# Four-layer network on one core: spilled and fresh expert pairs interleaved, fetched rows spread, gates in quarters, end of the layer and gmlp in a new order

## The chip, the cores and the metric

The kernel runs on one core of a Trainium2 chip. The metric is device time in microseconds (us) of one execution, as the median of several. A profiled execution of the same program gives the trace from which all rows below come. Engines are named as in the profile: PE is TensorE's matmul, PEld its weight load, DVE is VectorE, ACT is ScalarE, POOL is GpSimd, SP is SyncE, which here only starts transfers; a "q" behind a name is that engine's DMA queue.

## The reference

The network handles 512 tokens of width 1024 in fp32 through several layers. Two of its pieces matter. `peer` routes each token, by 8 heads and two sets of 128 sub-keys, to 16 experts a head; an expert's number is `i1 * 128 + i2`, and its first and second matrices are one row each of `expert_u` and `expert_v` (16384 rows).

```python
def peer(n, w_q, sub_keys_1, sub_keys_2, expert_u, expert_v):
    ...
        v1, i1 = lax.top_k(s1, PEER_TOPK)
        v2, i2 = lax.top_k(s2, PEER_TOPK)
        cand_s = (v1[..., :, None] + v2[..., None, :]).reshape(...)
        cand_i = (i1[..., :, None] * PEER_NKEYS + i2[..., None, :]).reshape(...)
        top_s, pos = lax.top_k(cand_s, PEER_TOPK)
        idx = jnp.take_along_axis(cand_i, pos, axis=-1)
        g = jax.nn.softmax(top_s, axis=-1)
        u_sel = jnp.take(expert_u, idx, axis=0)
        act = jax.nn.gelu(jnp.einsum('thkd,td->thk', u_sel, xc).astype(jnp.float32))
        v_sel = jnp.take(expert_v, idx, axis=0)
        return jnp.einsum('thk,thkd->td', (g * act).astype(xc.dtype), v_sel)
```

`gmlp_mixer` follows it in the next layer: `u = gelu(u_pre)`, `v = layer_norm(gelu(v_pre))`, `v` mixed over the tokens of a chunk by a lower-triangular matrix for each group, and `u * mixed` as the result.

## The kernel before

**Numbers and tiles.** Tokens stand in 4 blocks of 128. Each fp32 product is made of three matmuls on parts: `mm3` (L354 to L359) does hi x hi, lo x hi and hi x lo. Weights stream from HBM as 128 x 1024 tiles: SP starts the transfer into `raw` (3 buffers), ScalarE casts it to `whi` (L319), VectorE subtracts to `wlo` (L320); `whi` and `wlo` have 4 buffers each. `parts` (L486, L487) does the same for activations. The 16384 experts are handled as 128 tiles ("expert 0 to 127" below) of 128 rows each.

**Block 0's tokens are sparse.** For them each chosen row is fetched by an indirect DMA from POOL (L1429) into `row` (5 buffers, 4 fetches ahead), first from `u`, reduced against the token on VectorE (L1438), then from `v`, added into `acc` (L1446). There are 128 of each; `next(fetch)` advances this by one row.

**Blocks 1 to 3 (384 tokens) are dense.** Each of the 128 expert tiles is projected for all 384 tokens (24 matmuls of 384 columns into bank `pm` or `pt`), passed through gelu, multiplied by a dense table of gates `G` (mostly zeros), split into `zh` and `zl`, and multiplied by its tile of `w_v` into 6 banks (2 `pa`, 4 `pm`), 18 matmuls of 512 columns, which accumulate over all 128 experts.

**Leads.** While `peer_gates` works out scores, picks and gates, TensorE would have little to do, so `lead` projects the first LEAD = 104 experts there, and SP stores their gelu to a DRAM table `H` (a "spilled" expert). 102 of them are placed by a list of fill counts, the others by `while todo: lead()`. The picks (L1509 to L1512) find `ex`, the expert number of each of 16 picks among 50 candidates: `eq` compares, `oh` multiplies, `reduce_sum` adds over the candidates, which is here the axis with a step of 16 elements.

**The expert stage** (`peer_experts`) handles experts in pairs. `act(e)` loads gates for 8 experts at a time (1.5 MB, the first group in three parts), loads `zs` for four spilled experts at a time (768 KB, 2 buffers) or projects a fresh pair, and makes `zh`, `zl`. `out(e, b)` does the output matmuls. The loop does a pair's outputs, then `beside(3)` rows for a spilled pair and `beside(6)` for a fresh one, then `act(e + 4)`. Pairs 0 to 51 are spilled, 52 to 63 fresh.

**The end of the layer.** `end(b)` scales, norms (`two_norms`) and adds the residual for block b; `late[b]` transposes it (TensorE, L497), `behind` places these transpositions behind a block of `w3_gv` matmuls, and `begin(b)` starts those. In `gmlp` each of four rounds projects `u` (`fm`), takes its gelu, and mixes `v` by 128 x 128 matmuls (L1883) of `gmw`, for which POOL's `gmv` must be done.

**Order.** A scheduler sorts each engine's instructions ahead of time; an engine then runs them strictly in that order. A DMA started by ACT (`G`, `zs`) or SP (`raw`) waits in that engine's order for its buffer, and what stands behind it waits too.

Of the kernel before, what the change touches and what calls it, by code (L numbers as in the profile page):

```python
# [9 lines left out]
F32 = mybir.dt.float32  # L10
# [6 lines left out]
OP = mybir.AluOpType  # L17
# [268 lines left out]
class Builder:  # L286
# [169 lines left out]

    def tmb_block(self, st, x, ks, b, h, ps):
        n = len(ks)
        for i, k in enumerate(ks):
# [924 lines left out]
    def peer(self):  # L1384

        tc = self.tc
        GT, TS, NE, LEAD, N = 8, 16, 128, 104, S - P
        with tc.tile_pool(name="pe", bufs=1) as p0, tc.tile_pool(name="ped", bufs=1, space=DRAM) as pd, \
                ExitStack() as right:
            nT = self.nT  # L1390
            G = pd.tile([N // TS, P, NE, TS], F32, name="gates")
            H = pd.tile([LEAD // GT, P, GT, N], F32, name="lead")
            su = self.stream("w2_u")
            n0 = p0.tile([P, D], F32, name="n0")
            self.nc.sync.dma_start(n0, self.n0)
            with tc.tile_pool(name="pek", bufs=1) as p, tc.tile_pool(name="pet", bufs=2) as t2, \
                    tc.tile_pool(name="pey", bufs=2) as ty:

                todo = list(range(LEAD))

                def lead(i=0, n=1, fill=1):

                    r = None
                    for _ in range((i + 1) * fill // n - i * fill // n):
                        e = todo.pop(0)
                        z = p0.tile([P, N], F32, name="z", bufs=3)
                        ps = self.pm.tile([P, 512], F32, name="pm")
                        self.fm_half(su, e, nT, 8, ps, P, S)
                        r = self.nc.scalar.activation(z, ps[:, P:], AF.Gelu_apprx_tanh)
                        self.nc.sync.dma_start(H[e // GT, :, e % GT], z)  # L1410
                    return r
                fetch = self.peer_gates(p, t2, ty, p0, right, n0, nT, G, TS, NE, lead)
                while todo:
                    lead()
            with tc.tile_pool(name="pek", bufs=1) as p:
                self.peer_experts(p, nT, su, G, H, GT, TS, NE, LEAD, *fetch)

# [31 lines left out]
    def peer_gates(self, p, t2, ty, p0, right, n0, nT, G, TS, NE, lead):  # L1449
# [9 lines left out]
        v.tensor_copy(iob, iot[:, :, None].to_broadcast([P, NE, 2]))  # L1459
        ioc = p.tile([P, NC, 16], BF16, name="ioc")  # L1460
        v.tensor_copy(ioc, iot[:, 0:NC, None].to_broadcast([P, NC, 16]))

# [32 lines left out]
        def picks(b, fill, then=None):  # L1495
# [100 lines left out]

    def peer_experts(self, p, nT, su, G, H, GT, TS, NE, LEAD, pr, fetch):

# [4 lines left out]
        gf = self.rowload(p, "gf2", name="gf2")  # L1603
        acc, parts, left = {}, {}, [2 * P - 96]

        def beside(n):
            for _ in range(min(n, left[0])):
                next(fetch)
            left[0] = max(left[0] - n, 0)

        def act(e):

            if e % GT == 0:
                gt = act.gt = p.tile([P, N // TS, GT, TS], F32, name="G", bufs=2)
                for b in range(0, N // TS, 8 if e == 0 else N // TS):
                    c = b + 8 if e == 0 else N // TS
                    nc.scalar.dma_start(gt[:, b:c], G[b:c, :, e:e + GT, :].rearrange("b p e t -> p b e t"))
# [11 lines left out]
            v.tensor_tensor(z.rearrange("p k (b t) -> p k b t", t=TS), z.rearrange("p k (b t) -> p k b t", t=TS),  # L1629
                            act.gt[:, :, e % GT:e % GT + 2, :].rearrange("p b e t -> p e b t"), OP.mult)  # L1630
            hi, lo = (p.tile([P, 2, N], F32R, name=n, bufs=3) for n in ("zh", "zl"))
# [11 lines left out]

        act(0)
        act(2)
        for e in range(0, NE - 2, 2):
            for k in range(2):
                for b in range(1, NB):
                    out(e + k, b)
            beside(3 if e < LEAD else 6)  # L1650
            if e + 4 < NE:
                act(e + 4)
        beside(2 * P)

        ys = [t.rearrange("p b e t -> p (b e t)") for t in (p.tile([P, N // TS, GT, TS], F32, name="G", bufs=2)
                                                            for _ in range(2))]
        ys = [t[:, k * D:(k + 1) * D] for t in ys for k in range(2)]
        after = self.mod_norm(p, 0, 1, EPS3, ys, lambda: p.tile([P, 512], F32, name="q", bufs=2))
        load, begin = self.open_tmb("w3_gv", self.nT, range(8))
        late = []  # L1660

        def end(b):
            self.late = []
            late.append(self.late)
            for h in range(2):
# [3 lines left out]
                self.two_norms(b, h, ps, gf, EPS2, EPS3, ys[b], after.turn)  # L1669
        end(0)  # L1670
        self.behind(None, late[0])
        load(0), load(1)
        for b in range(1, NB):
            for e in (NE - 2, NE - 1):
                last = out(e, b)
                if b == NB - 1:
                    load(e - NE + 4)
            end(b)
        for b in range(1, NB):
            self.behind(begin(b - 1), late[b])  # L1680
        self.late = []
# [172 lines left out]
    def gmlp(self, q, hT, yT):  # L1854
# [504 lines left out]
```

## Time and profile before

| what | value |
|---|---|
| median of 3 runs | 3916.0 us (3914.04 to 3924.2) |
| profiled execution, its own time | 3914.44 us |
| its span in the trace | 3912.3 us, mean granted TensorE clock 0.973 |
| PE busy | 3672.4 us, 94% of the span, 18377 instructions |
| DVE busy | 2586.7 us, 66% |
| ACT busy | 1433.3 us, 37% |
| POOL busy | 598.4 us, 15% |
| chain that ended last | PE 66%, DVE 13%, DMA 9%, issue 7% |

The span is what the trace covers; the execution's own time is 2.1 us longer. Busy shares are means over stages with different limits. In the profile's 40 slices PE falls to 6 to 8 tenths between the 22nd and the 28th slice, about 2150 to 2740 us, which is the expert stage.

### The profile page before, as it was taken

To read this page: it belongs to the slowest core of one execution; us is meant where nothing else is said; L and a number is where in the kernel's file an instruction comes from. 1 tells how busy PE (TensorE), PEld (TensorE's weight loads), DVE (VectorE), ACT (ScalarE), POOL (GpSimd) and SP (SyncE) were. 2 spreads that over 40 slices of the span, in tenths; PEclk is the share of its full clock that TensorE was granted. 3 is DMA by queue.
4 is the path that set the end of the run, shared out by engine and by line. 5 is a ranking of instruction groups with operands and counts; after the bars stand their busy time and mean duration, and the time that the engine had idled before them with its cause. 6 is when DMAs were issued, how large, how long until landed. Compare 5 with 4: busy or idle time off the path is not lost.

```text
span 3912.3 us, 48482 instructions
## 1 busy us (share of the span) xinstructions
PE 3672.4 (94%) x18377; PEld 3101.9 (79%) x18377; DVE 2586.7 (66%) x4472; ACT 1433.3 (37%) x2122; POOL 598.4 (15%) x630
## 2 busy tenths in 40 slices
PE   8999999999999999999989687789998999999998
PEld 6777877777888888898989566678986787788887
DVE  5755748758645646999999677764457546755344
ACT  4422333323224633334546222233343334534231
POOL 1122100000000000254243444410001000010000
PEclk9999999999999999999999798899998999999999
DMA  4132433546233233289899998875432221133332
GB/s 154 65 100 82 124 96 111 177 127 191 81 97 97 92 98 113 89 282 320 306 351 377 363 338 313 321 271 171 145 108 84 84 73 55 49 94 95 97 97 76
DMA packets 221275, 622.20 MB, mean 159 GB/s; under 512 B 21052, under 2 KB 85165, under 8 KB 217841
## 3 DMA queue, kind: packets, MB, share of 16 engines
q1 hardware_dynamic: 120576, 398.18, 31.2%
q0 software_dynamic: 39776, 142.52, 10.1%
q10 hardware_dynamic: 60688, 78.40, 5.9%
q8 instruction: 144, 2.36, 0.2%
q14 instruction: 91, 0.74, 0.1%
HBM read 570.76 MB, written 48.26 MB: 158 GB/s over the span
## 4 chain that ended last, share of the span: by engine, by line
PE 66%; DVE 13%; DMA 9%; issue 7%; ACT 2%; POOL 2%; DVEq 0%; SPq 0%; POOLq 0%; ACTq 0%
PE pm L357 18%; PE pm L359 18%; PE pm L358 18%; DMA zs<-lead 4%; DVE wlo L320 3%; DMA raw<-in_w_up_dram 2%; DVE acc L1446 1%; POOL row L1429 1%; PE pa L358 1%; PE pa L359 1%; PE pt L359 1%; PE pt L357 1%; PE pt L358 1%; PE pa L357 1%; PE pt L497 1%
## 5 line engine op out<-in xcount | busy, mean ns | idle before, releaser
L319 ACT CAST whi<-raw 128x1024 fp32r<-128x1024 f32 x661 | 694.1, 1051 | 1617.0 <-PE pm L359 478.8
L320 DVE TENSOR_TENSOR wlo<-raw,whi 128x1024 fp32r<-128x1024 f32 x661 | 817.3, 1237 | 662.4 <-ACT whi L319 653.8
L357 PE MATMUL pm<-xTh,whi 128*128 128x512 f32 (+2 forms) x2784 | 1016.5, 366 | 35.1 <-ACT whi L319 21.0
L359 PE MATMUL pm<-xTh,wlo 128*128 128x512 f32 (+2 forms) x2784 | 1008.4, 363 | 13.4 <-DVE wlo L320 13.1
L358 PE MATMUL pm<-xTl,whi 128*128 128x512 f32 (+2 forms) x2784 | 1009.7, 363 | 2.2 <-DVE xTl L487 2.2
L357 PEld LDWEIGHTS pm<-xTh,whi 128*128 128x128 f32 x2784 | 531.1, 191 | 102.8 <-ACT whi L319 24.8
L359 PEld LDWEIGHTS pm<-xTh,wlo 128*128 128x128 f32 x2784 | 530.3, 191 | 82.2 <-DVE wlo L320 21.1
L358 PEld LDWEIGHTS pm<-xTl,whi 128*128 128x128 f32 x2784 | 531.7, 191 | 63.3 <-DVE xTl L487 2.8
L1429 POOL DMA_INDIRECT row<-in_u_rows_dram,rows x128 | 182.9, 1429 | 285.9 <-DVE row L1438 243.8
L1429 POOL DMA_INDIRECT row<-in_w_v_dram,rows x128 | 186.0, 1453 | 236.1 <-DVE acc L1446 208.4
L357 PE MATMUL pm<-whi,zh 128*128 128x512 f32 x512 | 204.3, 399 | 0.0
L358 PE MATMUL pm<-wlo,zh 128*128 128x512 f32 x512 | 203.1, 397 | 0.0
L359 PE MATMUL pm<-whi,zl 128*128 128x512 f32 x512 | 202.7, 396 | 0.0
L358 PE MATMUL pa<-wlo,zh 128*128 128x512 f32 x256 | 106.2, 415 | 71.4 <-DVE wlo L320 71.3
L1446 DVE SCALAR_TENSOR_TENSOR acc<-row,hw,acc 128x1024 f32<-128x1024 f32 x127 | 163.1, 1285 | 14.6 <-DMA row<-in_w_v_dram,rows 12.7
L357 PE MATMUL pm<-whi,xTh 128*128 128x512 f32 (+1 forms) x400 | 161.7, 405 | 7.3 <-ACT xTh L486 4.3
L1438 DVE SCALAR_TENSOR_TENSOR row<-row,n 128x1024 f32<-128x1024 f32 x128 | 154.4, 1219 | 18.5 <-DMA row<-in_u_rows_dram,rows 18.3
L359 PE MATMUL pm<-whi,xTl 128*128 128x512 f32 (+1 forms) x400 | 155.3, 389 | 0.0
L358 PE MATMUL pm<-wlo,xTh 128*128 128x512 f32 (+1 forms) x400 | 153.8, 385 | 0.0
L357 PE MATMUL pa<-whi,zh 128*128 128x512 f32 x256 | 101.9, 399 | 32.9 <-ACT zh L486 32.9
L358 PEld LDWEIGHTS pa<-wlo,zh 128*128 128x128 f32 x256 | 49.9, 195 | 89.9 <-DVE wlo L320 80.6
L1629 DVE TENSOR_TENSOR zs<-zs,G 128x768 f32<-128x768 f32 x52 | 47.5, 954 | 106.3 <-DMA zs<-lead 106.3
(652 smaller groups left out, 6330.7 us busy)
## 6 DMA issues: line engine op xcount, KB each, us to landing
raw<-in_w_v_dram SPq DMA_DIRECT2D x136, 512.0 KB, 6.7
raw<-in_w_u_dram SPq DMA_DIRECT2D x128, 512.0 KB, 4.9
raw<-in_w_m_dram SPq DMA_DIRECT2D x64, 512.0 KB, 3.5
raw<-in_w_up_dram SPq DMA_DIRECT2D x55, 512.0 KB, 3.5
raw<-in_w_ada_dram SPq DMA_DIRECT2D x48, 512.0 KB, 4.5
gates<-G ACTq DMA_DIRECT2D x24, 1024.0 KB, 7.5
G<-gates ACTq DMA_DIRECT2D x15, 1536.0 KB, 24.7
lead<-z SPq DMA_DIRECT2D x104, 192.0 KB, 6.1
```

The lines of the kernel that those rows point to most:

```text
L319: nc.scalar.copy(hi, src)
L320: (nc.gpsimd if u < self.aside else nc.vector).tensor_tensor(lo, src, hi.bitcast(F32), OP.subtract)
L357: mm(ps, lhsT=a[0], rhs=b[0], start=first, stop=False)
L358: mm(ps, lhsT=a[0], rhs=b[1], start=False, stop=False)
L359: return mm(ps, lhsT=a[1], rhs=b[0], start=False, stop=last)
L497: self.nc.tensor.transpose(ps[:, j, :], src[:, j * P:(j + 1) * P], self.ident)
L1429: nc.gpsimd.indirect_dma_start(r, None, tabs[e], bass.IndirectOffsetOnAxis(ap=idx[e][:, j:j + 1], axis=0))
L1438: v.scalar_tensor_tensor(r, r, 1.0, n0, op0=OP.mult, op1=OP.mult, accum_out=hs[:, j:j + 1])
L1446: v.scalar_tensor_tensor(acc, r, w[:, j:j + 1], acc, op0=OP.mult, op1=OP.add)
L1629: v.tensor_tensor(z.rearrange("p k (b t) -> p k b t", t=TS), z.rearrange("p k (b t) -> p k b t", t=TS), act.gt[:, :, e % GT:e % GT + 2, :] ...
```

## The change

- `lead` now covers 112 experts: all pairs n with n % 8 != 7 (`held`, 56 pairs). The 8 fresh pairs are 7, 15, ..., 63, one in each run of eight.
- `H` is stored and `zs` loaded by pairs (384 KB), `zs` in 6 buffers and three pairs ahead (`zload(e + 6)`). Gates of the next group of 8 experts come in four quarters over the group before (`gload`).
- The 160 rows of block 0 that are left for this stage are spread over pairs 0 to 59 by weights of 1 (spilled) and 2 (fresh). Block 0's `end(0)` stands at pair 60 in place of behind the loop.
- The three other `end(b)` stand behind all last outputs; each `begin(b)` is split in halves, and the transpositions of a block stand behind the first.
- `eq` and `oh` are laid out [16, candidates], so that the sum runs over neighbouring elements.
- `gmlp` does the four projections of `u` first, then the four mixes.

```diff
@@ begin, in open_tmb
-            return self.tmb_block(st, x, ks, b, 0, st.begun[b])
+            n = len(ks) // 2
+            yield self.tmb_block(st, x, ks, b, 0, st.begun[b], range(n))
+            self.tmb_block(st, x, ks, b, 0, st.begun[b], range(n, 2 * n))
...
@@ peer
-        GT, TS, NE, LEAD, N = 8, 16, 128, 104, S - P
+        GT, TS, NE, N = 8, 16, 128, S - P
+        held = [n for n in range(NE // 2) if n % 8 != 7]
...
-            H = pd.tile([LEAD // GT, P, GT, N], F32, name="lead")
+            H = pd.tile([len(held), P, 2, N], F32, name="lead")
...
-                todo = list(range(LEAD))
+                todo = [(k, n, c) for k, n in enumerate(held) for c in range(2)]
...
-                        self.nc.sync.dma_start(H[e // GT, :, e % GT], z)
+                        self.nc.sync.dma_start(H[k, :, c], z)
...
@@ peer_gates
-                eq = t2.tile([P, NC, 16], BF16, name="eq")
-                v.tensor_tensor(eq, ioc, tpf[:, h, None, :].to_broadcast([P, NC, 16]), OP.is_equal)
-                oh = t2.tile([P, NC, 16], F32, name="oh")
-                v.tensor_tensor(oh, eq, ci[:, h, :, None].to_broadcast([P, NC, 16]), OP.mult)
-                v.reduce_sum(ex[:, h, :], oh.rearrange("p c k -> p k c"), axis=AX.X)
+                eq = t2.tile([P, 16, NC], BF16, name="eq")
+                v.tensor_tensor(eq, ioc, tpf[:, h, :, None].to_broadcast([P, 16, NC]), OP.is_equal)
+                oh = t2.tile([P, 16, NC], F32, name="oh")
+                v.tensor_tensor(oh, eq, ci[:, h, None, :].to_broadcast([P, 16, NC]), OP.mult)
+                v.reduce_sum(ex[:, h, :], oh, axis=AX.X)
...
@@ peer_experts
+        def gload(e, n, c):
...
+            if e not in gts:
+                gts[e] = p.tile([P, N // TS, GT, TS], F32, name="G", bufs=2)
+            b = slice(N // TS // n * c, N // TS // n * (c + 1))
+            nc.scalar.dma_start(gts[e][:, b], G[b, :, e:e + GT, :].rearrange("b p e t -> p b e t"))
+
+        def zload(e):
+            if e // 2 in held:
+                zs[e] = p.tile([P, 2, N], F32, name="zs", bufs=6)
+                nc.scalar.dma_start(zs[e], H[held.index(e // 2)])
...
-            if e % GT == 0:
-                gt = act.gt = p.tile([P, N // TS, GT, TS], F32, name="G", bufs=2)
-                for b in range(0, N // TS, 8 if e == 0 else N // TS):
...
-            if e < LEAD:
-                if e % 4 == 0:
-                    act.zs = p.tile([P, 4, N], F32, name="zs", bufs=2)
-                    nc.scalar.dma_start(act.zs, H[e // GT, :, e % GT:e % GT + 4])
-                z = act.zs[:, e % 4:e % 4 + 2]
-            else:
+            g0 = e - e % GT
+            gload(g0 + GT, GT // 2, e % GT // 2)
+            zload(e + 6)
+            z = zs.pop(e, None)
+            if z is None:
...
-            beside(3 if e < LEAD else 6)
...
+        due = [0]
+        for e in range(0, NE - GT, 2):
+            due.append(due[-1] + (1 if e // 2 in held else 2))
+        rows = 2 * P - 96
...
+            n = e // 2
+            if n + 1 < len(due):
+                for _ in range(rows * due[n + 1] // due[-1] - rows * due[n] // due[-1]):
+                    next(fetch)
+            elif n + 1 == len(due):
...
+                ys = [pr.tile([P, D], F32, name="row", bufs=5) for _ in range(NB)]
+                after = self.mod_norm(p, 0, 1, EPS3, ys, lambda: p.tile([P, 512], F32, name="q", bufs=2))
+                end(0)
+                self.behind(None, late[0])
...
         for b in range(1, NB):
             for e in (NE - 2, NE - 1):
-                last = out(e, b)
+                out(e, b)
                 if b == NB - 1:
                     load(e - NE + 4)
+        for b in range(1, NB):
             end(b)
         for b in range(1, NB):
-            self.behind(begin(b - 1), late[b])
+            half = begin(b - 1)
+            self.behind(next(half), late[b])
+            for _ in half:
+                pass
...
@@ gmlp
+        us = []
         for n in range(4):
             pu = self.fm(st, n, hT, 8)
-            u = tmp()
-            self.gelu2(u, pu, tmp)
+            us.append(tmp())
+            self.gelu2(us[n], pu, tmp)
+        for n, u in enumerate(us):
             ps = self.pa.tile([P, NB, P], F32, name="pa")
```

**What it moves on the engines.** First VectorE where the expert stage begins: L1438 and L1442 reduce a fetched row of `u`, L1629 and L1636 multiply `zs` by the gates. Before:

```order
L1438 SCALAR_TENSOR_TENSOR row,hs<-row,n_11457 128x1024
L1444 TENSOR_SCALAR acc_13256<-row,hw 128x1024
L1446 SCALAR_TENSOR_TENSOR acc_13256<-row,hw,acc_13256 128x1024 x4
L1629 TENSOR_TENSOR zs<-zs,G 128x768 x3
L320 TENSOR_TENSOR wlo<-raw,whi 128x1024
L1629 TENSOR_TENSOR zs<-zs,G 128x768
```

After:

```order
L1442 SCALAR_TENSOR_TENSOR row,hs<-row,n_11457 128x1024 x3
L320 TENSOR_TENSOR wlo<-raw,whi 128x1024
L1636 TENSOR_TENSOR zs<-zs,G 128x768 x2
L320 TENSOR_TENSOR wlo<-raw,whi 128x1024
L1636 TENSOR_TENSOR zs<-zs,G 128x768
L1442 SCALAR_TENSOR_TENSOR row,hs<-row,n_11457 128x1024 x2
L320 TENSOR_TENSOR wlo<-raw,whi 128x1024
L490 TENSOR_TENSOR zl<-zs,zh 128x768
```

The weights' `wlo` of the last leads now stand between the first `zs` products and behind the first of them; before, one output weight stood there.

ScalarE at the same place: L1409 and L1413 are the leads' gelu, L1617 starts a transfer of gates, L1621 and L1622 one of `zs`. Before:

```order
L1409 ACTIVATE z<-pm 128x384
L319 CAST whi<-raw 128x1024
L1617 DMA G<-gates 128x8x128 x2
L1409 ACTIVATE z<-pm 128x384
L1617 DMA G<-gates 128x8x128
L1621 DMA zs<-lead 128x1536 x2
L319 CAST whi<-raw 128x1024
L1617 DMA G<-gates 128x24x128
```

After:

```order
L1617 DMA G<-gates 128x8x128 x2
L1413 ACTIVATE z<-pm 128x384
L319 CAST whi<-raw 128x1024
L1617 DMA G<-gates 128x8x128
L1622 DMA zs<-lead 128x768
L1413 ACTIVATE z<-pm 128x384
L319 CAST whi<-raw 128x1024
L1622 DMA zs<-lead 128x768 x2
L1413 ACTIVATE z<-pm 128x384
L319 CAST whi<-raw 128x1024
L1617 DMA G<-gates 128x6x128
L1622 DMA zs<-lead 128x768
```

Gelus and casts of leads now stand between the transfers that ScalarE starts.

TensorE at the first mix of `gmlp`: L357 to L361 are a projection of `u`, L1883 and L1910 the mix. Before, with 28 matmuls of the projection (`pm<-xTh,whi` and its two companions) ahead of it:

```order
L357 MATMUL pm<-xTh,whi 128x512
L358 MATMUL pm<-xTl,whi 128x512
L1883 MATMUL pa<-gmw,gmv 128x128 x2
L357 MATMUL pm<-xTh,whi 128x512
L358 MATMUL pm<-xTl,whi 128x512
L1883 MATMUL pa<-gmw,gmv 128x128 x4
L359 MATMUL pm<-xTh,wlo 128x512
```

After, with 6 ahead of it:

```order
L361 MATMUL pm<-whi,xTl 128x512
L359 MATMUL pm<-xTh,whi 128x512
L360 MATMUL pm<-xTl,whi 128x512
...
L1910 MATMUL pa<-gmw,gmv 128x128 x2
L361 MATMUL pm<-xTh,wlo 128x512
```

The first mix stands 22 matmuls of the projection earlier than it did.

## Rows read from the trace of the kernel before

**Rows 1.** The page's groups: the two preparations of a weight tile, whole span.

```profile
L319 ACT CAST whi<-raw 128x1024 fp32r<-128x1024 f32 x661 | 694.1, 1051 | 1617.0 <-PE pm L359 478.8
L320 DVE TENSOR_TENSOR wlo<-raw,whi 128x1024 fp32r<-128x1024 f32 x661 | 817.3, 1237 | 662.4 <-ACT whi L319 653.8
```

**Rows 2.** Windows: us, busy of PE, PEld, DVE, ACT, POOL, clock, DMA share, GB/s.

```profile
2020.00:2146.00 126.00, 120.62 (x948) 118.56 (x947) 124.22 (x193) 79.74 (x97) 42.61 (x32) 0.97 0.98 365
2155.00:2188.00 33.00, 0.12 (x1) 0.00 (x0) 13.65 (x17) 2.37 (x4) 10.98 (x11) 0.54 1.05 386
2188.00:2199.00 11.00, 6.31 (x15) 4.52 (x16) 10.89 (x11) 1.66 (x2) 4.84 (x3) 0.51 1.11 293
2199.00:2660.00 461.00, 389.65 (x1621) 313.88 (x1620) 333.36 (x304) 127.88 (x140) 170.36 (x116) 0.93 0.86 313
2660.00:2900.00 240.00, 240.00 (x1193) 215.56 (x1191) 100.44 (x99) 84.03 (x102) 1.79 (x6) 1.00 0.46 144
```

**Rows 3.** TensorE's waits, 2159 to 2700 us: waited for, us in total, times, longest.

```profile
PE pa L358 <- DVE wlo L320: 71.3, 20, 10.1
PE pa L357 <- ACT zh L486: 32.9, 1, 32.9
PE pa L359 <- DVE zl L487: 4.6, 1, 4.6
```

**Rows 4.** The spilled tile in DRAM, who waited for it: us, times.

```profile
  DVE zs L1629: 106.3, 21
```

**Rows 5.** Transfers from 2188 to 2660 us, then 2020 to 2146: count, KB, us to landing.

```profile
raw<-in_w_v_dram SPq DMA_DIRECT2D x90, 512.0 KB, 6.9
...
raw<-in_w_v_dram SPq DMA_DIRECT2D x4, 512.0 KB, 8.1
```

**Rows 6.** TensorE's timeline: start in us, duration, instruction, in brackets its wait.

```profile
2149.76 0.33 PE L357 MATMUL pm<-xTh,whi 128*128 128x384 f32 x1
2154.79 0.34 PE L359 MATMUL pm<-xTh,wlo 128*128 128x384 f32 x1
2188.06 0.77 PE L357 MATMUL pa<-whi,zh 128*128 128x512 f32 x1 [32.94 <-ACT zh L486]
2896.33 0.39 PE L357 MATMUL pa<-whi,zh 128*128 128x512 f32 x1
2904.31 0.39 PE L359 MATMUL pm<-whi,zl 128*128 128x512 f32 x1
2913.67 0.39 PE L357 MATMUL pa<-whi,xTh 128*128 128x512 f32 x1
```

**Rows 7.** Timeline of ScalarE's queue and of VectorE where the expert stage begins.

```profile
2160.12 12.50 ACTq L1617 DMA_DIRECT2D G<-gates  x1
2186.14 2.73 DVE L1629 TENSOR_TENSOR zs<-zs,G 128x768 f32<-128x768 f32 x3 [11.10 <-DMA zs<-lead]
```

**Rows 8.** Groups by line from 1600 to 2155 us: the three steps of the picks.

```profile
L1512 DVE TENSOR_REDUCE ex<-oh 128x16 f32<-128x800 f32 x32 | 49.4, 1548 | 0.0
L1511 DVE TENSOR_TENSOR oh<-eq,ci 128x800 f32<-128x800 bf16 x32 | 31.4, 987 | 0.0
L1509 DVE TENSOR_TENSOR eq<-ioc,tpf 128x800 bf16<-128x800 bf16 x32 | 18.2, 580 | 0.0
```

**Rows 9.** TensorE's timeline at the end of the layer and in `gmlp`.

```profile
2942.14 1.03 PE L497 MATMUL pt<-base,x 128*128 128x128 f32 x8
2967.86 1.23 PE L1883 MATMUL pa<-gmw,gmv 128*128 128x128 f32 x4 [6.03 <-POOL gmv L1874]
2994.93 1.05 PE L1883 MATMUL pa<-gmw,gmv 128*128 128x128 f32 x8
```

More of the change, by code (lines that the diff above doesn't have):

```diff
@@ L455, in tmb, with tmb_block @@
         self.late = []
-    def tmb_block(self, st, x, ks, b, h, ps):
+    def tmb_block(self, st, x, ks, b, h, ps, part=None):
         n = len(ks)
-        for i, k in enumerate(ks):
+        for i in part or range(n):
+            k = ks[i]
             a = (x[0][:, k, b * P:(b + 1) * P], x[1][:, k, b * P:(b + 1) * P])
@@ L1415, in peer @@
             with tc.tile_pool(name="pek", bufs=1) as p:
-                self.peer_experts(p, nT, su, G, H, GT, TS, NE, LEAD, *fetch)
+                self.peer_experts(p, nT, su, G, H, GT, TS, NE, held, *fetch)
     def peer_rows(self, p0, pr, n0, idx, gate):
@@ L1459, in peer_gates @@
         v.tensor_copy(iob, iot[:, :, None].to_broadcast([P, NE, 2]))
-        ioc = p.tile([P, NC, 16], BF16, name="ioc")
-        v.tensor_copy(ioc, iot[:, 0:NC, None].to_broadcast([P, NC, 16]))
+        ioc = p.tile([P, 16, NC], BF16, name="ioc")
+        v.tensor_copy(ioc, iot[:, None, 0:NC].to_broadcast([P, 16, NC]))
         val = [p.tile([P, NB, 8, 16], F32, name=f"val{e}") for e in range(2)]
@@ L1595, in peer_gates, with peer_experts @@
         return pr, fetch
-    def peer_experts(self, p, nT, su, G, H, GT, TS, NE, LEAD, pr, fetch):
+    def peer_experts(self, p, nT, su, G, H, GT, TS, NE, held, pr, fetch):
         nc, v = self.nc, self.nc.vector
@@ L1603, in peer_experts @@
         gf = self.rowload(p, "gf2", name="gf2")
[L1604 to L1609, printed above, removed]
[L1611 to L1623 removed]
+        acc, parts, gts, zs = {}, {}, {}, {}
+        def gload(e, n, c):
+            if e >= NE:
+                return
+            if e not in gts:
[6 more added lines that the diff above has]
+                nc.scalar.dma_start(zs[e], H[held.index(e // 2)])
+        def act(e):
+            g0 = e - e % GT
[3 more added lines that the diff above has]
+            if z is None:
                 z = p.tile([P, 2, N], F32, name="z2", bufs=2)
@@ L1642, in out @@
             return last
[L1644 to L1649, printed above, removed]
-            beside(3 if e < LEAD else 6)
[L1651 to L1659, printed above, removed]
         late = []
@@ L1669, in end @@
                 self.two_norms(b, h, ps, gf, EPS2, EPS3, ys[b], after.turn)
-        end(0)
-        self.behind(None, late[0])
+        for c in range(3):
+            gload(0, 3, c)
+        for e in range(0, 6, 2):
+            zload(e)
+        act(0)
+        act(2)
+        due = [0]
+        for e in range(0, NE - GT, 2):
+            due.append(due[-1] + (1 if e // 2 in held else 2))
+        rows = 2 * P - 96
+        for e in range(0, NE - 2, 2):
+            for k in range(2):
+                for b in range(1, NB):
+                    out(e + k, b)
+            n = e // 2
[3 more added lines that the diff above has]
+            elif n + 1 == len(due):
+                for _ in fetch:
+                    raise AssertionError("rows")
+                ys = [pr.tile([P, D], F32, name="row", bufs=5) for _ in range(NB)]
+                after = self.mod_norm(p, 0, 1, EPS3, ys, lambda: p.tile([P, 512], F32, name="q", bufs=2))
+                end(0)
+                self.behind(None, late[0])
+            if e + 4 < NE:
+                act(e + 4)
+        load, begin = self.open_tmb("w3_gv", self.nT, range(8))
         load(0), load(1)
@@ L1674, in peer_experts @@
             for e in (NE - 2, NE - 1):
-                last = out(e, b)
+                out(e, b)
                 if b == NB - 1:
                     load(e - NE + 4)
+        for b in range(1, NB):
             end(b)
         for b in range(1, NB):
-            self.behind(begin(b - 1), late[b])
+            half = begin(b - 1)
+            self.behind(next(half), late[b])
+            for _ in half:
+                pass
         self.late = []
```

10 lines of the change are left out of this document (5 added, 5 removed).

## The prediction

> **What bounds the kernel now.** I read the busy time by stretch first [rows 2], then who made TensorE wait in the expert stage [rows 3], then what held the engine that it waited for [rows 4, 5]. TensorE is the bottleneck wherever it is fed. From 2660 to 2900 us, where fresh pairs run, it is busy 240.0 of 240 us at clock 1.00 and the DMA engines are only 0.46 busy. From 2199 to 2660 us, where spilled pairs run, the DMA share is 0.86 and TensorE is busy 389.65 of 461 us at clock 0.93 [rows 2]. So the work is unevenly mixed: one half lacks transfer time, the other has it to spare.
>
> What TensorE waits for there is VectorE's `wlo`, 71.3 us in 20 waits [rows 3]. VectorE works in order and stood in front of the `zs` product, waiting 106.3 us for the spilled tile to land [rows 4]. Ahead of that is one long stop: 2154.79 is the last lead matmul, 2188.06 the first expert output matmul [rows 6], and the waits give 32.9 us to it [rows 3]. In it the DMA engines move 386 GB/s [rows 2].
>
> How much can be won in the stage at most? Two matmul pitches at full clock come from starts. Outputs: 2896.33 to 2904.31 is 35 steps, 0.228 us each. A 384-column projection: 2149.76 to 2154.79 is 29 steps, 0.1735 us [rows 6]. The stage from 2154.79 to 2913.67 (the first matmul of the next projection [rows 6]) takes 758.9 us. Its work is 64 pairs x 36 x 0.228 = 525.3 us, plus 24 fresh experts x 24 x 0.1735 = 99.9 us, plus 1.0 us for block 0's eight transpositions (a group of eight takes 1.03 [rows 9]): 626 us. **133 us are lost**: 33 in the stop, about 100 behind it (76 are listed waits, the rest is the slower clock after them: 0.51 from 2188 to 2199, 0.93 after [rows 2]).
>
> **The change part by part.**
>
> *More leads ahead of the experts.* 112 instead of 104 experts are projected early. That moves 8 x 24 x 0.1735 = 33.3 us of TensorE work from the stage's end into the stop; total work is the same. What the stop then costs is read from the orders. Before it, weights for three more experts already stood prepared (they were the first output weights); the eight new leads take them. The last three leads have their `wlo` behind VectorE's first `zs` product, and that ran at 2186.14 for want of its tile [rows 7]. So: products at 2186.1, next `wlo` done at about 2188.8, three leads at 4.16 us, first output at about 2201.5. From 2155 that is 46.5 us for 33.3 us of work, 13 lost. The transfers in it also grow by eight weight tiles of 0.524 MB, 4.2 MB, 11 us at 386 GB/s. And the first 11 us behind the stop run at 0.51, about the lower level of 1.2 GHz [rows 2], which costs about 5 us; I keep that. ScalarE's queue gets worse: gelus and casts of the leads stand between its DMA issues, one of which held it 12.50 us [rows 7]; behind it wait the casts of the next leads, and behind the gelus the stores and weight loads on SP. Bounds: 14 lost (chain alone) to 40. I take 13 + 11 + 5 = 29.
>
> *Interleaved pairs, rows spread.* One group is now seven spilled pairs and one fresh one. Its TensorE time is 8 x 36 x 0.228 + 48 x 0.1735 = 74.0 us. Its bytes: 18 weight tiles of 0.524 MB, seven `zs` of 0.393, gates 1.573, and 160 rows x 9/67 = 21.5 rows of 0.524: 25.0 MB, or 338 GB/s. Before, four spilled pairs took 32.8 us of TensorE work and 8 weight tiles, 12 rows, gates and two `zs`: 13.6 MB, 415 GB/s, over the 313 GB/s achieved and the 365 that the busiest long stretch moved at share 0.98 [rows 2]. Now 338 lies between the two, so it depends on the latency of each transfer. `zs` is loaded three pairs (25 us) ahead, where it now comes 5.1 us late (106.3 / 21 waits [rows 4]); gates arrive in quarters over a group. I put the `zs` wait at nothing: its cover is those 25 us, and it comes back if a landing takes longer.
>
> What is late next is the weights. Both kinds of pair use one tile in about 4.13 us (18 x 0.228 or 24 x 0.1735), through three `raw` buffers. One round is landing + cast + subtraction + what stands ahead on VectorE. With the landing of the same tiles under load, 8.1 us [rows 5], cast 1.05, `wlo` 1.24 and two operations ahead of 1.2 us [rows 1], it is 12.8 us, 4.27 us a tile: 0.14 us too slow, x 144 tiles = 20 us. Bounds: 0 (the fresh stretch, none lost [rows 2]) to 47 (the stage keeps 313 GB/s: 25.0 MB take 79.9 us, 5.9 more x 8 groups). The stretch from 2020 to 2146, share 0.98, lost 5 of 126 us [rows 2], 4%, which of 592 us would be 25: near 20, which I take. The order puts a fresh pair's projection one output pair (8.2 us) ahead of its use; its gelu, product, cast and subtraction take about 4 us, so they are hidden. Rows get rarer (2.4 a pair, not 3), so POOL's queue gets lighter.
>
> Sum for the stage: 133 - (29 + 20) = **84 us won**.
>
> *The reduction's layout* in the top-16 picks, 32 times each. `reduce_sum` reads 800 elements with a stride and takes 1.548 us; `oh`, also 800 elements, takes 0.987 us [rows 8]. Read in order it should come to about the latter: -0.56. Against that, `eq` now takes 0.580 us [rows 8] and its second operand becomes a repeated element: bounds 0.58 to 0.99. Both ends: -18 to 0 us of VectorE time in all (32 x 0.56, and with `eq` at 0.99, 32 x 0.15 = 5 won). I take `eq` at `oh`'s 0.99: 5 us of VectorE time, some 3 on the path, since VectorE is nearly full there (124.22 of 126 in the neighbouring stretch [rows 2]) but TensorE is as well.
>
> The row behind that choice shows `eq` at 0.580 us for 800 elements, about half of `oh`. The Trainium skill, "VectorE: DVE Perf Modes", section "What auto-detection actually checks", says that the double rate needs 16-bit tensors with step +-1 in every operand; the new operand repeats. By that rule `eq` loses its rate and the edit wins 5 us of VectorE time; without it 18. No row here shows a repeated 16-bit operand.
>
> *End of the layer.* Now: from 2913.67 to the last transposition at 2942.14 [rows 6, 9] are 28.5 us for 72 matmuls (16.4) and two groups of transpositions of 1.03 (2.1). In the new order 60 matmuls stand ahead of it (13.7 + 2.1), and with 2 us of waiting for the norm it starts at about 2931.5. From there to the first `gmw` matmul is a chain of ScalarE, VectorE and POOL, 2967.86 - 2942.14 = 25.7 us; a `wlo` of 1.2 us no longer stands in it: 24.5. But the new order has this matmul behind 42 others (9.6 us) where it had 52, so **TensorE waits about 14 us there**, more than the 6.0 of now [rows 9]; the gmlp edit turns one wait into another. It comes at 2931.5 + 24.5 = 2956. After it 95 matmuls run without a wait on POOL: 21.6, the small `gmw` ones 2.1 (8 take 1.05 [rows 9]), and 5 for a start at the slower clock as after the stop. The end of this piece comes at 2984.8, with six matmuls more done (1.4), against 2994.93 + 1.05: **13 us won**. Bounds 3 to 20: if the norm's chain sets the pace the first part wins nothing; if the gates' chain shortens with it, more.
>
> Block 0's norm moves from behind the pairs into them; it is VectorE and ScalarE work (about 10 us) beside TensorE's fresh pair, hidden as now. Stores in pairs of 384 KB instead of 768 KB change no byte.
>
> Total: 84 + 3 + 13 = 100. The profiled execution took 3914.4 us (span 3912.3), 1.6 below the median of the runs: 3914.4 - 100 + 1.6 gives about **3816 us**.
>
> **The rivals.** *Nearly nothing is lost* (0.2): start 18, pairs 0: 133 - 18 + 16 = 131, 3785 us. For it: no wait at all from 2660 to 2900. Against: share 0.46 there.
>
> *Transfers bound the whole stage* (0.2): 313 GB/s as now and a start of 40: lost 87, won 46 + 16 = 62, 3854 us; with 293 GB/s (2188 to 2199 [rows 2]) 25.0 MB take 85.3 us, 90 + 40 lost, 3897 us. For it: landings of 8 us and more at high share. Against: 365 GB/s from 2020 to 2146.
>
> *Slower: the weight ring keeps its pace* (0.07). Place: the three `raw` buffers in the pairs. Now 90 tiles take 472 us [rows 5], 5.24 us a tile. If that is the ring and not the `zs` wait, it now holds for all 144 tiles, the interleaved fresh ones too, which today run at 4.29: (5.24 - 4.13) x 144 = 160, + 29 at the start, against 133 lost now, less 16: 3957 us. It decides from 4.96 us a tile: (133 + 16 - 29) / 144 + 4.13. Against it: TensorE's waits name `wlo`, and VectorE's queue stood for `zs`.
>
> *It does not do what it says* (0.03): the `zs` product runs ahead but the queue stops for a late quarter of the gates instead; four such stops a group of 2.6 us (8 groups, 84 us) would eat the gain of the stage: about 3900.
>
> **How the numbers follow.** Forecast 0.5, rivals as above. About 0.3% (12 us) is what a measurement of this kernel can tell from no change. Faster 0.90 (forecast, lossless, transfer bound), same 0.03, slower 0.07. The range leaves out the slower case, the "does not" case and the upper half of the transfer case, 0.2 in all; its upper end is the middle of that case: 3783 to 3875.
>
> **What would show it.** Right: the stop after the last gate matmul filled by leads, under 20 us of TensorE idle before the first output; `zs` gone from VectorE's waits; a group in 74 to 79 us at 315 to 340 GB/s; `ex` near 1.0 us and `eq` near 1.0; one wait of some 14 us for `gmv`, none after. Wrong: `wlo` waits over 50 us in the pairs, ScalarE's casts waiting for `raw` with TensorE behind them, or a group over 82 us.

## The result, and the profile after

The changed kernel takes 3864.7 us (median; 3864.5 to 3867.7), the kernel before 3915.4 beside it: a ratio of 0.987, interval 0.985 to 0.989. 51 us are won where 100 were forecast. The time lies within the stated range, at its far end, among the cases that the prediction called bound by transfers. The profiled execution has a span of 3862.9 us against 3912.3, so 49.4 us are to be found in the trace.

TensorE's timeline of the changed kernel (start, duration, instruction, in brackets its wait): last gate matmul, last lead, first output matmul, first `w3_gv` matmul, last transposition, first and last mix.

```profile
2118.05 0.62 PE L1589 MATMUL pa<-o,r 128*128 128x128 f16 x8
...
2174.87 0.33 PE L361 MATMUL pm<-xTh,wlo 128*128 128x384 f32 x1
2175.05 0.40 PE L359 MATMUL pa<-whi,zh 128*128 128x512 f32 x1
...
2875.64 0.39 PE L359 MATMUL pa<-whi,xTh 128*128 128x512 f32 x1
...
2898.21 1.03 PE L500 MATMUL pt<-base,x 128*128 128x128 f32 x8
2918.06 1.22 PE L1910 MATMUL pa<-gmw,gmv 128*128 128x128 f32 x4 [5.60 <-POOL gmv L1899]
...
2944.61 1.16 PE L1910 MATMUL pa<-gmw,gmv 128*128 128x128 f32 x8
```

These answer [rows 6, 9]; the last gate matmul of the kernel before started at 2146.10. Four pieces follow from them. "Lost" is a piece's length less its work by the pitches of the prediction; the first pair (21.8 us for 8.2; 15.9 before) counts with the start, since part of it runs at the lower clock.

| piece | won, predicted | won, measured | working |
|---|---|---|---|
| up to the last gate matmul | 3 | 28.0 | 2146.10 - 2118.05 |
| start, first pair with it | 29 left lost | 29.0 left lost, 12.3 won | 57.0 - 10 leads x 4.164, + 13.6; before 33.6 + 7.7 |
| pairs behind it | 20 left lost | 94 left lost, 2 given away | 700.6 - 592.9 - 13.6; before 725.6 - 626.2 - 7.7 |
| first `w3_gv` matmul to last mix | 13 | 12.2 | (2995.98 - 2913.67) - (2945.77 - 2875.64) |

28.0 + 12.3 - 2.4 + 12.2 is 50.1; 0.7 goes again behind. So the start and the end came as reckoned in their sums, the pairs won nothing, and the piece up to the last gate matmul, which had been given 3 us, holds more than half of the result.

Windows of the changed kernel (us, busy of PE, PEld, DVE, ACT, POOL, clock, DMA share, GB/s): the leads in the former stop, the first 32 pairs, the others.

```profile
2120.00:2175.00 55.00, 44.47 (x233) 42.45 (x232) 34.70 (x48) 14.47 (x22) 22.49 (x19) 0.91 1.04 383
2175.00:2580.00 405.00, 326.14 (x1347) 265.66 (x1346) 303.47 (x274) 103.57 (x118) 187.52 (x125) 0.90 0.91 326
2580.00:2860.00 280.00, 280.00 (x1284) 237.56 (x1284) 135.75 (x139) 100.54 (x117) 1.66 (x6) 1.00 0.58 189
```

The stop is filled: TensorE is busy 44 of 55 us where it was 0.12 of 33 [rows 2]. But the stage is as uneven as before. The first half of the pairs runs at 326 GB/s, share 0.91, clock 0.90; in the second TensorE does not wait at all and the transfers are at 0.58. A group of eight pairs takes 104, 100, 99 and 102 us in the first half, and 73.7 in the second, the pure work (74.8 for the last group, with block 0's transpositions). VectorE's additions of fetched rows (line L1450, busy in us and count) show why:

```profile
2175.00:2580.00 405.00, 163.48 (x127) 0.90 0.91 326
2580.00:2875.00 295.00, 0.00 (x0) 1.00 0.57 185
```

All 127 additions fall into the first 32 pairs: about 32 a group, none in the second half. The rows are not spread. What VectorE waits for from 2159 to 2800 us (waited for, us, times, longest) answers [rows 4]; `zs` is better, 65.6 us for 106.3, and gates took its place:

```profile
DVE zs L1636 <- DMA G<-gates: 68.9, 8, 10.8
DVE zs L1636 <- DMA zs<-lead: 65.6, 25, 5.0
DVE wlo L320 <- ACT whi L319: 41.8, 19, 2.9
```

And TensorE's waits in the same stretch, beside [rows 3]:

```profile
PE pa L360 <- DVE wlo L320: 28.7, 9, 10.7
PE pt L361 <- DVE wlo L320: 17.2, 3, 7.2
PE pa L359 <- ACT zh L489: 16.8, 4, 5.4
PE pm L359 <- ACT z L1413: 9.9, 2, 5.5
```

### The profile page after: what moved, and what is told of

The parts are those of the page before. It is cut to its first block, busy times and chain, and to the rows that moved or that the text cites. A ratio compares the mean times of both kernels' runs of the same rounds, so it can differ in the third digit from the quotient of the medians.

```text
span 3862.9 us, 48601 instructions
## 1 busy us (share of the span) xinstructions
PE 3671.0 (95%) x18377; PEld 3101.3 (80%) x18377; DVE 2583.8 (67%) x4472; ACT 1434.0 (37%) x2122; POOL 609.8 (16%) x630
## 4 chain that ended last, share of the span: by engine, by line
PE 66%; DVE 14%; DMA 9%; issue 7%; ACT 2%; POOL 2%; ACTq 0%; DVEq 0%; SPq 0%; POOLq 0%
PE pm L359 18%; PE pm L361 18%; PE pm L360 18%; DVE wlo L320 3%; DMA raw<-in_w_up_dram 2%; DMA row<-in_w_v_dram,rows 2%; DMA zs<-lead 2%; DVE row L1442 1%; PE pa L359 1%; PE pa L361 1%; PE pa L360 1%; POOL row L1433 1%; DVE r L1582 1%; PE pt L500 1%; ACT whi L319 1%
## 5 line engine op out<-in xcount | busy, mean ns | idle before, releaser
L359 PE MATMUL pm<-xTh,whi 128*128 128x512 f32 (+2 forms) x2848 | 1037.8, 365 | 43.7 <-ACT whi L319 30.0
L361 PE MATMUL pm<-xTh,wlo 128*128 128x512 f32 (+2 forms) x2848 | 1029.4, 362 | 13.6 <-DVE wlo L320 11.3
L360 PE MATMUL pm<-xTl,whi 128*128 128x512 f32 (+2 forms) x2848 | 1032.3, 363 | 2.2 <-DVE xTl L490 2.2
L359 PEld LDWEIGHTS pm<-xTh,whi 128*128 128x128 f32 x2848 | 543.2, 191 | 112.1 <-ACT whi L319 34.4
L361 PEld LDWEIGHTS pm<-xTh,wlo 128*128 128x128 f32 x2848 | 543.0, 191 | 81.8 <-DVE wlo L320 20.8
L360 PEld LDWEIGHTS pm<-xTl,whi 128*128 128x128 f32 x2848 | 544.3, 191 | 63.3 <-DVE xTl L490 3.0
L361 PE MATMUL pm<-whi,zl 128*128 128x512 f32 x512 | 201.9, 394 | 0.0
L1450 DVE SCALAR_TENSOR_TENSOR acc<-row,hw,acc 128x1024 f32<-128x1024 f32 x127 | 163.5, 1287 | 10.2 <-DMA row<-in_w_v_dram,rows 8.5
L1442 DVE SCALAR_TENSOR_TENSOR row<-row,n 128x1024 f32<-128x1024 f32 x128 | 153.4, 1217 | 12.8 <-DMA row<-in_u_rows_dram,rows 12.7
L361 PE MATMUL pm<-whi,xTl 128*128 128x512 f32 (+1 forms) x400 | 154.1, 386 | 0.0
L1636 DVE TENSOR_TENSOR zs<-zs,G 128x768 f32<-128x768 f32 x56 | 53.3, 956 | 140.6 <-DMA G<-gates 68.9
L359 PEld LDWEIGHTS pm<-whi,zh 128*128 128x128 f32 x512 | 98.8, 193 | 32.3 <-ACT z L1413 11.1
L359 PE MATMUL pa<-whi,zh 128*128 128x512 f32 x256 | 103.3, 404 | 20.3 <-ACT zh L489 16.8
```

What stands on the lines that cost most here:

```text
L359: mm(ps, lhsT=a[0], rhs=b[0], start=first, stop=False)
L360: mm(ps, lhsT=a[0], rhs=b[1], start=False, stop=False)
L361: return mm(ps, lhsT=a[1], rhs=b[0], start=False, stop=last)
L1442: v.scalar_tensor_tensor(r, r, 1.0, n0, op0=OP.mult, op1=OP.mult, accum_out=hs[:, j:j + 1])
L1450: v.scalar_tensor_tensor(acc, r, w[:, j:j + 1], acc, op0=OP.mult, op1=OP.add)
```

## The experiments

**Rows tied to the pairs (e1), and left out (e2).** The program text asks for rows by `due`, but nothing holds VectorE's work on them back: the scheduler is free to put it earlier, and did. e1 holds it.

```diff
+            los[e] = v.tensor_tensor(lo, z, hi.bitcast(F32), OP.subtract)
...
+                with self.tc.issue_after(los[e + 2].ins):
+                    for _ in range(rows * due[n + 1] // due[-1] - rows * due[n] // due[-1]):
+                        next(fetch)
```

> The changed kernel with one addition: the reductions of block 0's fetched rows are issued behind VectorE's zl subtraction of the pair after next, so that the rows really spread to pair 59. In the changed kernel they run at about 31 a group of eight pairs and are used up after pair 35; there a group takes 99 to 104 us, later ones 74. Theory T (transfers: 18 weight tiles of 0.524 MB, 7 zs of 0.393, gates 1.573 and 31 rows of 0.524 are 30.0 MB a group, at 320 GB/s 94 us): with 21.5 rows a group it is 25.0 MB, 78 us at 320 GB/s, in all eight groups, 8 x 4 = 32 us lost in place of 105: about 3865 - 73 = 3792 us, 3785 to 3815. Rival Q (what costs is the queues: VectorE standing for G and zs whenever rows are beside, whatever their number): 20 us or more lost in each of eight groups, 160 and more in place of 105, so 3865 + 55 = 3920 us.

Measured: 3785.4 us (3781.8 to 3796.8), ratio 0.968, interval 0.966 to 0.970. That is 79 us less than the changed kernel. L1450 again (the stage of e1 ends at 2793.3, within the second window), and TensorE's waits from 2159 to 2800 us, of e1:

```profile
2175.00:2580.00 405.00, 99.93 (x78) 0.97 0.91 326
2580.00:2875.00 295.00, 62.77 (x49) 0.96 0.66 232
```

```profile
PE pa L360 <- DVE wlo L320: 24.7, 8, 6.3
PE pt L361 <- DVE wlo L320: 2.4, 1, 2.4
```

In the same 405 us, with the same 326 GB/s, 78 additions run in place of 127, and the clock is 0.97 in place of 0.90. Counted with the reductions of rows from `u` (28 against 1) and the first row of `v`, it is 107 rows in place of 129. From the first output to the first `w3_gv` matmul it takes 633.9 us where the changed kernel took 700.6. Theory T holds: the queues alone would have cost every group.

Some 15 of the 79 us come ahead of the first output, which neither theory had. The rows had run ahead under the leads too: the reductions (L1442, two records each) from 2120 to 2175 us, in the changed kernel and in e1, are 17 and 4.

```profile
2120.00:2175.00 55.00, 20.69 (x34) 0.91 1.04 383
2120.00:2175.00 55.00, 4.74 (x8) 1.00 1.02 354
```

With the same ten leads, e1 takes 42.1 us from the last gate matmul to the first output (2117.31 to 2159.45) for 41.6 of work, where the changed kernel took 57.0, and its first pair takes 9.5 us for 21.8.

In e2 the loop that calls `next(fetch)` is empty.

> The changed kernel without the rows of block 0 that are fetched in the expert stage (160 fetches and their VectorE work are left out, block 0 gets zeros for this term). Theory T: the weights, zs and gates of a group are 13.8 MB, 186 GB/s at TensorE's pace, so the pairs lose almost nothing: every group 74 us, 3865 - 105 = about 3760 us. Rival Q (late quarters of the gates and late zs by the order of ScalarE's queue): VectorE still stands for G and zs and groups stay above 85 us, 3820 us or more.

Measured: 3738.8 us, a single run; seven groups take 73.7 us, the last 74.8, and TensorE waits for nothing in the pairs. (The bytes in both expectations lack 1.57 MB a group: eight pairs hold 16 experts, so two loads of gates. e2 moves 210 GB/s in the pairs, 15.5 MB a group, not 13.8.)

**Transfers or VectorE's work (e11, e12).** e2 took both away. e11 keeps the transfers and cuts VectorE's work on the rows:

```diff
-                v.scalar_tensor_tensor(acc, r, w[:, j:j + 1], acc, op0=OP.mult, op1=OP.add)
+                v.scalar_tensor_tensor(acc[:, 0:64], r[:, 0:64], w[:, j:j + 1], acc[:, 0:64], op0=OP.mult, op1=OP.add)
```

> e1_rows_tied with every transfer as it is, but VectorE's work on the 160 rows that are fetched in the expert stage cut from 1024 to 64 columns (the other 960 columns of those rows are left out of the result). e2 took the transfers and VectorE's work away together, so it can't say which of them costs. With 31.75 rows a group, as in the changed kernel, VectorE's work is 18 x 1.24 + 16 x 0.95 + 31.75 x 1.28 = 78 us for 74 of TensorE, with 20 rows 63: it is near full too. Theory T (bytes): the pairs lose 30 to 43 us as in e1, within 15 us of e1's time. Rival V (VectorE's row work): under 10 us lost, about 3745 us, as without rows.

Measured: 3839.5 us, a single run, slower than e1 by 54, seven groups of 85 to 89 us. V's number is missed by 95 us, and T's too. With cheaper rows the scheduler had made another order, in which the additions stand in bunches of up to four (in e1 118 of 128 stand alone), and VectorE now waits for the fetched rows themselves (2150 to 2860 us):

```profile
DVE zs L1637 <- DMA zs<-lead: 107.0, 30, 8.9
...
DVE acc L1451 <- DMA row<-in_w_v_dram,rows: 52.0, 25, 5.2
```

e1 has 9.3 us for that row. e12 therefore takes the transfers away and leaves VectorE's order as in e1, row for row:

```diff
+            if n < 96:
                 nc.gpsimd.indirect_dma_start(r, None, tabs[e], ...)
+            else:
+                nc.gpsimd.memset(r, 0.0)
```

> e1_rows_tied with each of the 160 fetches of the expert stage replaced by a fill with zeros of the same buffer by POOL (those rows are left out of the result). VectorE keeps the order and the work that it has in e1, instruction for instruction; only the transfers of 0.524 MB each are gone. e11, which kept the transfers and cut VectorE's work, got slower than e1 (3839.5, 87 us a group), but VectorE's order had changed with it. Theory T (the transfers): the pairs lose nothing, 74 us a group, as in e2, about 3740 us. Rival V (VectorE's work and its order are enough to hold TensorE): groups of 78 us and more as in e1, 3770 us or more.

Measured: 3737.2 us, a single run, seven groups of 73.7 us and a last one of 74.8. The window of the first half in e12:

```profile
2175.00:2580.00 405.00, 405.00 (x1846) 342.74 (x1845) 332.37 (x335) 141.34 (x154) 112.43 (x117) 1.00 0.67 210
```

VectorE is busier than in the changed kernel (332 us for 303), in e1's order, and TensorE does not wait once. So it is the rows' transfers that cost in the pairs. For the 15 us ahead of the first output, no run separates the transfers from VectorE's work.

**The same tie in the kernel before (e5).** No interleaving, 2 rows a spilled pair and 5 a fresh one.

```diff
-            beside(3 if e < LEAD else 6)
+            with self.tc.issue_after(los[e + 2].ins):
+                beside(2 if e < LEAD else 5)
```

> The kernel before (spilled pairs first, fresh ones last, gates and zs loaded as before) with block 0's rows tied to the pairs as in e1_rows_tied, 2 a spilled pair and 5 a fresh one, in place of 3 and 6 untied. It tells whether the interleaving is needed at all. Theory T (only bytes a stretch count): four spilled pairs move 8 weight tiles and 8 rows of 0.524 MB, gates 1.573 and two zs of 0.786: 11.5 MB, 36.5 us at 316 GB/s for 32.8 us of work, 3.7 lost x 13 = 48; a fresh pair 5.1 MB in 16.5 us, 310 GB/s, none lost; the stop of 33 stays. 81 lost in place of 133: 3916 - 52 = 3864 us (3850 to 3880). Rival I (the interleaving, the deeper zs and the quarters are what frees the stage): the zs waits stay and nothing is won, 3905 to 3916 us.

Measured: 3860.7 us, ratio 0.986, interval 0.985 to 0.988; T had 3864. This edit by itself wins as much as the whole change, although VectorE still waits 102.4 us for `zs`. T's number came out by luck in part: the stop that T left at 33 us shrank to 14 (the first output comes 22.6 us behind the last gate matmul, for 8.3 of leads), while 12.5 us that T did not have are lost between the last output and the first `w3_gv` matmul, where TensorE waits 8.3 us for block 0's norm behind the last rows.

**Interleaving by itself (e10).** e1 with `held = list(range(56))`.

> e1_rows_tied with the 112 spilled experts as the first 56 pairs and the 8 fresh pairs last, everything else as in e1: what the interleaving is worth by itself once the rows are tied. Four spilled pairs then move 8 weight tiles and 10 rows of 0.524 MB, gates 1.573 and four zs of 0.393, 12.6 MB in 32.8 us of work, 383 GB/s. Theory T (bytes of a stretch): at 345 GB/s, the best of e1's stretches, 36.5 us, 3.7 x 14 = 51 us lost, at 316 98, against 43 lost in e1: 3793 to 3840, I take 3820 us. Rival E (only the sum of bytes over the stage counts, or the waits are elsewhere): 3785 us within 8.

Measured: 3803.2 us (3801.7 to 3808.3), 18 us over e1. Between the two: the interleaving is worth 18 us once rows are tied, T's 35 is too much.

**Gates in thirds (e6) and products held back (e9).** Both go after the 69 us that VectorE waits for gates in e1.

```diff
-            gload(g0 + GT, GT // 2, e % GT // 2)
+            if e % GT < 6:
+                gload(g0 + GT, 3, e % GT // 2)
```

> e1_rows_tied with the gates of the next eight experts loaded in thirds beside the first three of four pairs, in place of quarters beside all four. In e1 VectorE waited 69.2 us in 9 waits for gates where a new eight begins, and TensorE 28.1 us in the pairs, nearly all behind wlo; the pairs lost 43 us in all. Theory G (it is the last quarter, issued one pair ahead of its use): gates gone from VectorE's waits but for the first group, some 30 of the 43 us back, 3755 us. Rival B (bytes: 24.7 MB a group at 316 GB/s are 78 us, whichever transfer is late): another wait takes its place, 3785 us, within 8.

Measured: 3789.3 us; the wait for gates stayed (75.4 us in 10), so it decides nothing on G. e9 puts each product behind the `zl` of the pair before:

```diff
+            with self.tc.issue_after(los[e - 2].ins) if e >= 2 else nullcontext():
                 v.tensor_tensor(z.rearrange(...), z.rearrange(...), gts[g0][...], OP.mult)
```

> e1_rows_tied, and each product of zs (or z) with its gates issued behind VectorE's zl of the pair before, so that it no longer runs up to three pairs ahead. In e1 and e6 the gates' buffer comes free with the last product of the group that holds it, at 2521 us in e1; the four quarters are issued by 2527.6, and the products of the next pairs, which stand ahead of the fresh pair's wlo on VectorE, wait until 2542.6, once in eight pairs. Theory P (the stop is these early products in VectorE's order, not bytes): gates below 30 of 69 us in VectorE's waits, 15 to 30 of the 43 us lost in the pairs back, 3765 us. Rival B (bytes): 3785 us within 8. Rival Z (zh comes too late for TensorE, since the product, cast and subtraction of 2.8 us then stand close ahead of its use): TensorE waits for zh or zl in most pairs, 3800 us or more.

Measured: 3782.2 us (3778.9 to 3787.0). VectorE's waits in e9, 2150 to 2800 us:

```profile
DVE wlo L320 <- ACT whi L319: 103.3, 54, 8.1
DVE zl L1641 <- ACT zh L1640: 55.4, 27, 9.8
DVE row L1442 <- DMA row<-in_u_rows_dram,rows: 2.8, 1, 2.8
```

Gates and `zs` are gone from the list altogether, and the time is the same within 3 us: rival B's number. In their place VectorE waits for the cast of a weight tile, 103.3 us for 66.0, and for `zh`, 55.4 for 7.8; TensorE's waits from 2159 to 2800 us sum to 27.8 us, in e1 to 28.1. The first half moves 329 GB/s, hardly more than e1's 326:

```profile
2175.00:2580.00 405.00, 392.38 (x1748) 328.00 (x1747) 310.80 (x313) 133.37 (x144) 168.68 (x109) 0.98 0.93 329
```

A wait named by the trace was removed in full and nothing was won. That the transfers behind it set the pace fits this row; but the tie brought the wait for `zh` with it, and no run separates the two.

**The picks' layout alone (e3), and undone (e4).**

> The kernel before with the layout of eq, oh and their sum alone changed. VectorE wins 32 x (1.548 + 0.580 + 0.987 - 0.977 - 0.992 - 0.989) = 5.0 us. The changed kernel ended its last gate matmul 28 us earlier (2118.05 against 2146.10). Theory V (VectorE's 5 us is all that the layout brings, the other 23 come from the order of the work there, which the other edits moved): 3911 us. Rival L (the layout brings the 28 by itself, since the picks stand ahead of what TensorE waits for): 3888 us.

Measured: 3907.3 us, ratio 0.998, interval 0.997 to 0.999: 8.6 won, nearer to V's time than to L's. But its last gate matmul comes at 2120.78, 25.3 earlier than before, as L said, and the first output 25.8 earlier; the first `w3_gv` matmul, though, comes only 7.9 earlier. The fetches of rows from `w_v` in e3 (min, median, max ns, then first and last start in us) show where it went:

```profile
L1429 POOL DMA_INDIRECT row<-in_w_v_dram,rows x128: 935/1678/1867, 2170.2 to 2596.7; - x128
```

In the kernel before the last of them started at 2577.8. The stage that began 25 us earlier fetched its rows until 19 us later, at 318 GB/s. It had more of them left: at the first output 127 of the 256 fetches had started in e3, and 138 in the kernel before, where these lines stand for all up to 2188.06 us:

```profile
L1429 POOL DMA_INDIRECT row<-in_u_rows_dram,rows x128: 932/1447/5346, 1675.1 to 2152.4; - x128
L1429 POOL DMA_INDIRECT row<-in_w_v_dram,rows x10: 932/937/1679, 2154.6 to 2175.3; - x10
```

The eleven rows of 0.524 MB are 18 us at 318 GB/s, by estimate, and 18 of the 25 us were given back.

> The changed kernel with the old layout of eq, oh and their sum. Theory V: 5 us slower, 3870 us, and the last gate matmul ends near 2123. Rival L: 28 us slower, 3893 us, last gate matmul near 2146.

Measured: 3888.1 us (3878.7 to 3890.8), 23 slower, near L's 3893; last gate matmul at 2142.80, 24.8 later, and 15 of it left at the first `w3_gv` matmul of the profiled execution. Both ways the layout is worth 25 us at the last gate matmul. VectorE's time for the three steps changed by 5.0 only, as reckoned. The steps in the changed kernel, beside [rows 8]:

```profile
L1513 DVE TENSOR_TENSOR eq<-ioc,tpf 128x800 bf16<-128x800 bf16 x32 | 31.6, 992 | 0.0
L1515 DVE TENSOR_TENSOR oh<-eq,ci 128x800 f32<-128x800 bf16 x32 | 31.5, 989 | 0.0
L1516 DVE TENSOR_REDUCE ex<-oh 128x16 f32<-128x800 f32 x32 | 31.1, 977 | 0.0
```

The rest is TensorE's waits from 1600 to 2146 us, 32.6 us before and 12.9 in e3, and the clock behind them. The three long ones of the kernel before (6.96 and 6.33 us for `r`, 5.38 for `gf`) are gone. VectorE's order changed too: ahead of the `r` that TensorE waited 6.96 us for, ten reductions of fetched rows stand between two steps of the gates before, and two in e3. (TensorE's own order is nearly the same in both, 32 gate matmuls between leads.) How much of the 20 us is the 5 us of VectorE and how much the other order was not separated.

**gmlp's old order (e7) and the old end of the layer (e8).**

> The changed kernel with gmlp's rounds in the old order (project, gelu, mix, four times). The prediction put a wait of 14 us ahead of the first mix and 13 us won in all at the layer's end and in gmlp; measured are 5.6 and about 12 (2913.67 to 2995.98 was 82.3 us, 2875.64 to 2945.77 is 70.1). Theory: the old order brings back the later waits for gmv (2.75 and 0.98 in the kernel before) and their slower clock, about 5 us: 3870 us. Rival: the new order brings nothing, TensorE's waits only stand elsewhere, 3865 us.

Measured: 3873.2 us (3868.3 to 3884.2), 8.5 slower, where the theory had 5; the piece from the first `w3_gv` matmul to the last mix is 74.1 us for 70.1, 4 of it. In the profiled execution that `w3_gv` matmul itself comes 6.6 us later, ahead of everything that this edit touches; why stays open.

> The changed kernel with the old end of the layer (each block's end behind its own outputs, transpositions behind a whole block of w3_gv). From the first w3_gv matmul to the last transposition of the blocks it took 28.5 us before and 22.6 in the changed kernel. Theory: the half blocks carry this difference, 6 us: 3871 us. Rival: the norms' chain on ScalarE and VectorE sets the pace and not the matmuls ahead, 3865 us.

Measured: 3880.2 us (3878.5 to 3883.8), 15.4 slower, which neither the 6 us of the theory nor the rival had; the same piece takes 84.7 us (82.3 before). The first mix comes 53.8 us behind the first `w3_gv` matmul (54.2 before, 42.4 changed), so the reordered end carries nearly all of the way to the mix, and the new order in `gmlp` pays only behind it.

## Why the prediction was off, point by point

- **Rows spread: the step that failed.** The prediction took "160 rows x 9/67 = 21.5 rows" a group from the program's table, and from it "338 GB/s". VectorE's order of the changed kernel says otherwise: 127 of the 256 rows are done at the first output, where the table has 96, and then stand 29, 31, 32, 32, 3, 0, 0, 0 additions ahead of the eight fresh products in turn. With 32 rows and two loads of gates (the prediction also counted one too few) a group is 32 MB; at 313 to 326 GB/s that is 98 to 102 us, the groups' 99 to 104. "20 lost" became 94. e1, with the rows really spread, lost 41 us from the first output to the end of the stage (633.9 - 592.9), the first pair with it. That is twice the 20: with two loads of gates a group has 26.6 MB, which at e1's 326 GB/s is 82 us for 74 of work.
- **"`zs` at nothing".** Wrong as a wait (65.6 us). It was not the price: e5 wins 52 us with 102.4 us of it left, and e9 wins nothing by being rid of it and of the gates' wait.
- **The weights' ring, 0.14 us too slow a tile.** Not a limit by itself: with the three `raw` buffers unchanged, the pairs without row transfers lost nothing (e12). What made a tile late under load is the transfers again. The 8.1 us of landing were those of four tiles; in the changed kernel's first half 67 tiles of `w_v` take 6.6 us.
- **The start, 29.** Measured 29.0, by luck: 15.4 ahead of the first output, one wait of 8.8 us for a lead's weight among them, and 13.6 in the first pair, two waits of 4.4 and 5.5 us for a lead's gelu among them. The 13 for the chain and the 11 for the leads' transfers were not what it cost: e1 has the same leads and loses 0.5 and 1.3 us there. The rows that ran ahead cost it, the same step that failed in the pairs.
- **The layout, "5 us of VectorE time, some 3 on the path".** The first half was exact; the path got 25 (e3, e4). This term was put too small by 22 us, and without the layout the change would have won about 23 us less (e4). `eq` took the upper bound, 0.992 us. The Trainium skill's rule in "VectorE: DVE Perf Modes", section "What auto-detection actually checks", told this rightly, and the trace agrees: with a repeated operand the 0.580 us of [rows 8] are gone.
- **The end, 13.** 12.2, with the parts otherwise: the wait for `gmv` is 5.6 us, not 14. The last transposition starts 22.6 us behind the first `w3_gv` matmul, not 17.8, so less is waited for afterwards; the chain from there is 19.9 us, not 24.5. The sum to the first mix, 42.4, is what was forecast (2956 - 2913.67), since the two errors cancel: luck, too.
- **The rivals.** "Transfers bound the whole stage" gave 3854 to 3897 and holds the measured time, but transfers bounded only the first half of the stage. The second half had transfer time to spare, and this is what e1 could use. The slower weights did not come.

So two errors ran against each other: 74 us too much hoped for in the pairs, 25 too little in the picks. That the time still lay in the range owes something to this.

The kernels with tied rows beat both, 3785.4 us (e1) and 3782.2 us (e9); the latter's ratio is 0.966, interval 0.965 to 0.968.

## What to carry to other kernels

Where a scheduler orders the engines, a table in the program that spreads work is only a wish: count, in the engine's own order, what stands between two marks, and tie it with an ordering edge if it has run ahead. In a stretch at some 320 GB/s, count its bytes before its waits: removing the named wait won nothing (e9), and work saved ahead of it was mostly given back (18 of 25 us in e3), since fetches that had run beside that work came behind it. To tell a transfer's cost from that of the work on its data, fill the buffer another way and keep the engine's order (e12), since an edit of the work alone moves the order (e11).

## What the runs showed of the hardware

The transfer queues cost unequally for a byte here. In the first half of the pairs of the changed kernel (2180 to 2590 us; packets, MB, share of 16 engines) the rows are q0, the weights q1, gates and `zs` q10:

```profile
q0 software_dynamic: 18102, 65.77, 43.0%
q1 hardware_dynamic: 11280, 40.10, 26.6%
q10 hardware_dynamic: 32978, 26.21, 20.8%
```

That is 0.65% and 0.66% of the stretch for a MB of rows or weights, and 0.79% for the gates and `zs`, whose packets are the smallest (0.8 KB on average, 3.6 for the rows). In this stretch rows fetched by index are no dearer for a byte than streamed weights. And a sum over 50 elements with a step of 16 took 1.548 us [rows 8], over neighbours 0.977.
